# An emitter's engine clocks with GpSimd's hold on VectorE, new task priorities in the first mixer, and a last product in a place of its own

## The chip, the cores and the metric

One core of a Trainium2 chip runs the whole kernel. The metric is device time in microseconds for one execution, lower is better. The core has five engines with instruction streams of their own, each in order: TensorE (PE in the profile, its weight loads PEld), VectorE (DVE), ScalarE (ACT), GpSimd (POOL) and SyncE (SP), which issues the DMAs.

## What is computed

A trunk of two layers on an input of 512 tokens by 1024 channels, float32. Layer 0 mixes tokens by four mLSTM heads and an S5 state space side by side, layer 1 by HGRN2; each layer ends in a SwiGLU channel mixer. Cut to what matters:

```python
for layer in range(2):
    h = rmsnorm(x, norm_g[layer, 0])
    mix = mixer_ab(h) if layer == 0 else mixer_c(h)
    x = x + rmsnorm(mix, norm_g[layer, 1])
    h = rmsnorm(x, norm_g[layer, 2])
    x = x + rmsnorm((silu(h @ w1) * (h @ w3)) @ w2, norm_g[layer, 3])

def mixer_ab(x):                                  # width 1024 -> 512 mLSTM, 512 gate, 512 S5
    xm, zm, us = split(x @ w_in)
    xc = silu(causal_dwconv(xm, conv_w, conv_b))
    q, k, v = blockwise(xc, wq), blockwise(xc, wk), blockwise(xm, wv)
    gates = concat(q, k, v) @ w_if + b_if
    out_m = (norm(mlstm(q, k, v, gates)) * mh_gain + skip * xc) * silu(zm)
    y = gelu(s5_ssm(us))                          # complex diagonal state space over positions
    out_s = y * sigmoid(y @ w_glu + b_glu)
    return concat(out_m, out_s) @ w_out

def mixer_c(x):
    q, f, i, g = split(x @ w_in)                  # 4 x 1024
    fg = lb + (1 - lb) * sigmoid(f)
    o = hgrn2(silu(q), 1 - fg, i, log(fg))        # 8 heads of 128, chunks of 64
    return (norm(o) * g_gain * silu(g)) @ w_out
```

## The kernel before

Everything stays in SBUF; weights stream in through SP's queue as `wraw` (512 KB a piece) and are split on the chip: ScalarE rounds `wraw` to `wh` (fp32r), VectorE or GpSimd makes `wl = wraw - wh`. Activations are split the same way into a high and a low part (`xh`, `xl`; `yh`, `yl`; `gh`, `gl`), and each product is three fp32r matmuls (high by high, low by high, high by low) of 128x512 into one PSUM bank. PSUM has four `bmm` banks, two `bs` and two `bm`, used in rotation.

The program runs mixer 0 (to about 231 us of the trace), SwiGLU 0 with its output phase (to about 616), mixer 1 (to about 880), SwiGLU 1, and a short tail. The parts overlap through tasks.

What sets the order is a Python emitter, class `Sched`. Each part of the program is a generator task with a priority number. The emitter keeps one modelled clock for each engine in `fr`; `mm`, `tp`, `tt`, `ts`, `stt`, `scan` and `act` emit one instruction and advance a clock by a cost written in them (`_go`). The next task is the one with the smallest key of three: the later of its wake time and the modelled PE clock, then its priority, then its wake time. `S.spawn(gen, wake, prio)` starts a task, `yield S.on(engine, t)` puts one back until an engine's clock has come near, `S.signal` and a yielded key tie tasks together. So costs and priorities together fix the order of the instructions on every engine, and with it which PSUM bank and which buffer each one has. `main()` has the lowest priority: the big projections `bmm<-xh,wh` and its two partners fill TensorE where nothing else is due. They are called the filler here. `Weights.task` asks the clocks of VectorE and GpSimd which of the two makes a `wl`.

In mixer 0 the names are these. `s5_setup` builds the S5 constants, `toeplitz` the kernel `TT` from `tts` (matmuls `bs<-p,tts` and copies). `s5_main` takes the four channel groups in turn: `bs<-X,WB` on PE, rotations and scans on VectorE (`t<-bs,Y` and on, ending in `xi` and `xr`), then a block of matmuls `X,TT`, `xr,WC`, `xi,WC` into one `bmm` bank, called the output block of a group here, and on ScalarE a gelu (`X<-bmm`), `yh`, and on VectorE `yl`. `mlstm` with its inner `head(h)` makes for each head a mask (`bmm<-negm,idb`, `bmm<-n,xh`), an Exp on ScalarE (`xh<-bmm`), and the score products (`bm<-xl,xc`). The GLU is the product `bmm<-yh,wh` and its partners. `post` normalises the mLSTM's chunks, `skip` and `evac` finish the results.

At the end of each phase the rows' mean squares go over PE (`bm<-mean,n`) to VectorE (`rstat`), to a power -0.5 on GpSimd (`rcol<-rstat,mhalf`), and by transposes back (`bm<-p,rcol`). In `last_out`, the end of SwiGLU 1, the closures made by `ev` evacuate the last sum as `Y`, ScalarE squares it with a row sum (`n<-Y`), VectorE multiplies `Y` by the gain in place (`Y<-Y,gb`), and a last `stt` makes `xh = Y * rcol + x`, which goes out by DMA.

## Time and profile before

| | |
|---|---|
| runs, us | 1236.94, 1237.29, 1232.99; median 1236.94 |
| the profiled execution, us | 1233.26; its span in the trace 1231.2 |
| mean granted TensorE clock | 0.991 |
| TensorE busy, us | 1197.5 (97 % of the span) |
| VectorE busy, us | 715.0 (58 %) |
| ScalarE busy, us | 524.6 (43 %) |
| GpSimd busy, us | 94.4 (8 %) |

Busy is time with an instruction running. The waits view says how long an engine stood idle ahead of a group of instructions, and which instruction of which engine ended that; the windows view gives busy time of each engine in a stretch and the granted TensorE clock (1.00 is the upper of its two levels, 2.4 GHz, 0.50 the lower, 1.2 GHz); the timeline lists instructions in order of start, with the idle time just ahead of each in brackets.

### The profile page before, as it was taken

To read this page: it belongs to the slowest core of one execution; us is meant where nothing else is said; L and a number is where in the kernel's file an instruction comes from. 1 tells how busy PE (TensorE), PEld (TensorE's weight loads), DVE (VectorE), ACT (ScalarE), POOL (GpSimd) and SP (SyncE) were. 2 spreads that over 40 slices of the span, in tenths; PEclk is the share of its full clock that TensorE was granted. 3 is DMA by queue.
4 is the path that set the end of the run, shared out by engine and by line. 5 is a ranking of instruction groups with operands and counts; after the bars stand their busy time and mean duration, and the time that the engine had idled before them with its cause. 6 is when DMAs were issued, how large, how long until landed. Compare 5 with 4: busy or idle time off the path is not lost.

```text
span 1231.2 us, 17078 instructions
## 1 busy us (share of the span) xinstructions
PE 1197.5 (97%) x6871; PEld 1016.0 (83%) x6871; DVE 715.0 (58%) x1206; ACT 524.6 (43%) x821; POOL 94.4 (8%) x96
## 2 busy tenths in 40 slices
PE   9998899999999999999999999999999999999997
PEld 8866789988888888889978787889888888888886
DVE  7999685963344434445876647755861454235533
ACT  5685575543423213233566455646541333024311
POOL 3100010000000000000122223310000000000000
PEclk9998899999999999999999999999999999999999
DMA  6301015132333322333042132222241243025301
GB/s 230 102 21 36 2 35 164 68 122 83 120 92 97 103 91 97 103 91 116 19 131 72 61 97 69 86 86 87 90 167 52 86 154 121 18 75 160 125 18 52
DMA packets 33902, 110.67 MB, mean 90 GB/s; under 512 B 3744, under 2 KB 4128, under 8 KB 33824
## 3 DMA queue, kind: packets, MB, share of 16 engines
q1 hardware_dynamic: 33824, 109.59, 27.5%
q8 instruction: 54, 0.88, 0.3%
q14 instruction: 24, 0.20, 0.1%
HBM read 107.47 MB, written 2.10 MB: 89 GB/s over the span
## 4 chain that ended last, share of the span: by engine, by line
PE 80%; DVE 13%; ACT 3%; issue 1%; POOL 1%; DMA 0%; SPq 0%; DVEq 0%; POOLq 0%; ACTq 0%
PE bmm L158 76%; PE bm L158 2%; DVE wl L178 2%; PE bs L158 2%; DVE t L178 2%; DVE n L178 1%; PE bm L162 1%; DVE n L190 1%; ACT wh L172 1%; DVE Y L178 1%; DVE t L194 1%; DVE xc L190 1%; POOL rcol L180 1%; ACT L170 1%; DMA wraw<-in_W_dram 0%
## 5 line engine op out<-in xcount | busy, mean ns | idle before, releaser
L158 PE MATMUL bmm<-xh,wh 128*128 128x512 f32 (+1 forms) x1008 | 383.5, 380 | 0.7 <-DVE Y L178 0.7
L158 PE MATMUL bmm<-xl,wh 128*128 128x512 f32 (+1 forms) x1008 | 378.8, 376 | 0.4 <-DVE xl L190 0.4
L158 PE MATMUL bmm<-xh,wl 128*128 128x512 f32 (+1 forms) x1008 | 378.6, 376 | 0.0
L172 ACT ACTIVATE wh<-wraw 128x1024 fp32r<-128x1024 f32 (+2 forms) x181 | 182.9, 1013 | 360.7 <-PE bmm L158 249.0
L178 DVE TENSOR_TENSOR wl<-wraw,wh 128x1024 fp32r<-128x1024 f32 (+2 forms) x180 | 211.3, 1176 | 100.4 <-ACT wh L172 99.8
L158 PEld LDWEIGHTS bmm<-xh,wh 128*128 128x128 f32 x1008 | 190.9, 189 | 34.6 <-issue 2.3
L158 PEld LDWEIGHTS bmm<-xh,wl 128*128 128x128 f32 x1008 | 190.9, 189 | 34.3
L158 PEld LDWEIGHTS bmm<-xl,wh 128*128 128x128 f32 x1008 | 191.0, 190 | 33.2 <-DVE xl L190 0.8
L178 DVE TENSOR_TENSOR a<-bmm,n 128x512 f32<-128x512 f32 x86 | 59.0, 690 | 184.3 <-PE bmm L158 182.1
L178 DVE TENSOR_TENSOR Y<-bmm,Y 128x512 f32<-128x512 f32 (+1 forms) x36 | 22.7, 630 | 94.7 <-PE bmm L158 94.7
L158 PE MATMUL bmm<-gh,wh 128*128 128x512 f32 (+1 forms) x160 | 60.6, 379 | 0.0
L158 PE MATMUL bmm<-gl,wh 128*128 128x512 f32 (+1 forms) x160 | 60.5, 378 | 0.0
L158 PE MATMUL bmm<-gh,wl 128*128 128x512 f32 (+1 forms) x160 | 60.5, 378 | 0.0
L180 POOL TENSOR_TENSOR rcol<-rstat,mhalf 128x2 f32<-128x2 f32 (+1 forms) x10 | 11.7, 1172 | 498.1 <-DVE rstat L186 498.1
L158 PE MATMUL bmm<-woh,gh 128*128 128x512 f32 x120 | 46.9, 391 | 0.0
L158 PE MATMUL bmm<-woh,gl 128*128 128x512 f32 x120 | 46.7, 389 | 0.0
L158 PE MATMUL bmm<-wol,gh 128*128 128x512 f32 x120 | 46.7, 389 | 0.0
L172 ACT ACTIVATE a<-a 128x512 f32<-128x512 f32 x44 | 27.4, 623 | 34.5 <-DVE a L178 34.3
L172 ACT ACTIVATE gh<-a 128x512 fp32r<-128x512 f32 x44 | 27.6, 631 | 33.2 <-DVE a L178 32.6
L172 ACT ACTIVATE xh<-X,p 128x256 fp32r<-128x256 f32 (+1 forms) x56 | 29.9, 537 | 26.2 <-DVE X L178 23.9
L170 ACT ACT_TABLE_LOAD x28 | 35.9, 1283 | 0.5
L158 PEld LDWEIGHTS bmm<-gh,wh 128*128 128x128 f32 x160 | 30.1, 188 | 5.7
(369 smaller groups left out, 1923.0 us busy)
## 6 DMA issues: line engine op xcount, KB each, us to landing
wraw<-in_W_dram SPq DMA_DIRECT2D x179, 512.0 KB, 3.5
wraw<-in_W_dram SPq DMA_DIRECT2D x18, 256.0 KB, 2.7
X<-in_x_dram SPq DMA_DIRECT2D x16, 256.0 KB, 4.2
wraw<-in_W_dram SPq DMA_DIRECT2D x8, 384.0 KB, 3.0
out_dram<-xh SPq DMA_DIRECT2D x8, 256.0 KB, 2.0
setb<-in_s5bc_dram SPq DMA_DIRECT2D x1, 512.0 KB, 5.7
gb<-in_gb_dram SPq DMA_DIRECT2D x1, 512.0 KB, 3.3
p<-in_p_dram SPq DMA_DIRECT2D x1, 226.5 KB, 5.6
```

The source lines that it names most:

```text
L158: self.nc.tensor.matmul(out, lhsT=lhsT, rhs=rhs, start=start, stop=stop, skip_group_check=True)
L162: self.nc.tensor.transpose(out, in_, ident)
L170: self.nc.scalar.preload_act_table_set(t)
L172: self.nc.scalar.activation(out=out, in_=in_, func=func, scale=scale, bias=bias)
L178: self.nc.vector.tensor_tensor(out=out, in0=in0, in1=in1, op=op)
L180: self.nc.gpsimd.tensor_tensor(out=out, in0=in0, in1=in1, op=op)
L190: self.nc.vector.scalar_tensor_tensor(out=out, in0=in0, scalar=scalar, in1=in1, op0=op0, op1=op1)
L194: self.nc.vector.tensor_tensor_scan(out, d0, d1, 0.0, op0, op1)
```

## The change

First, the emitter's model. VectorE instructions with both operands in SBUF (`held`) are modelled to end only after a GpSimd instruction that would run beside them. An fp32r matmul right behind one that is not fp32r, or behind a transpose, costs 0.087 us more. GpSimd's `tt`, power and `ts` have new costs. Second, priorities of mixer 0's tasks have new numbers. Third, in `last_out` the product goes to `z`, a tile of its own, and the last `stt` reads `z`; the square still reads `Y`.

```diff
@@ class Sched
+        self.hold = []
+        self.dense = True
-    def _go(self, eng, after, cost):
+    def _go(self, eng, after, cost, held=False):
         s = max(self.fr[eng], after, self.w)
         if eng == "v" and cost < 0.15 and after == 0.0:
             cost += 0.06
+        if held:
+            for a, b in self.hold:
+                if a < s + cost - 0.1 and s < b:
+                    s = max(s, b - cost + 0.1)
         self.fr[eng] = s + cost
+        if eng == "g" and cost > 0.3:
+            self.hold = self.hold[-7:] + [(s, s + cost)]
@@ mm, tp
-        return self._go("pe", after, p * n / 2300.0 if lhsT.dtype != F32R else n * 0.000428 + 0.0085)
+        cost = p * n / 2300.0 if lhsT.dtype != F32R else n * 0.000428 + 0.0085
+        if lhsT.dtype == F32R and not self.dense:
+            cost += 0.087
+        self.dense = lhsT.dtype == F32R
+        return self._go("pe", after, cost)
...
+        self.dense = False
@@ tt, ts, stt
-            return self._go("v", after, n / 960.0 + 0.07)
+            return self._go("v", after, n / 960.0 + 0.07, held=not (self.psum(in0) or self.psum(in1)))
-        return self._go("g", after, n * (0.00176 if op == ALU.mult and len(in0.shape) > 2 else 0.0022) + (0.2 + 0.17 * n if op == ALU.pow else 0.1))
+        return self._go("g", after, 0.35 + 0.17 * n + (0.4 if n == 4 else 0.0) if op == ALU.pow else n * 0.0024 + 0.1)
-        ... if eng == "v" else n * 0.00096 + 0.1)
+        ... if eng == "v" else n * 0.0026 + 0.1)
@@ last_out
+                z[i, f] = self.pt(f"xl{2 * i + f}")
-                t = S.tt(y, y, self.gb[:, 512 * f:512 * f + 512], ALU.mult, after=t)
+                S.tt(z[i, f], y, self.gb[:, 512 * f:512 * f + 512], ALU.mult, after=t)
...
-                t1 = S.stt(o, self.Y[:, 2 * i + f], r[:, 2:3], px[f][0], ALU.mult, ALU.add, after=t)
+                t1 = S.stt(o, z[i, f], r[:, 2:3], px[f][0], ALU.mult, ALU.add, after=t)
@@ mixer 0, the priorities that differ in value
-        S.spawn(self.rotations(fp), wake=S.fr["v"], prio=1)
+        S.spawn(self.rotations(fp), wake=S.fr["v"], prio=1.05)
-            S.spawn(turn(z, t), wake=t, prio=2)
+            S.spawn(turn(z, t), wake=t, prio=1.5)
-        S.cur[1] = 0.95
-        S.spawn(self.toeplitz(), prio=0.9)
+        S.cur[1] = 0.6
+        S.spawn(self.toeplitz(), prio=0.85)
-        S.spawn(values(), prio=0.8)
-        S.spawn(queries(), prio=1.15)
+        S.spawn(values(), prio=1.0)
+        S.spawn(queries(), prio=0.9)
-        S.spawn(head(0), prio=1.2)
-        S.spawn(head(1), prio=1.2)
+        S.spawn(head(0), prio=0.95)
+        S.spawn(head(1), prio=0.6)
-                    S.spawn(head(h), prio=1.2)
+                    S.spawn(head(h), prio=1.15)
-            S.spawn(self.post(fp, i, pn, po, gate[:, i], t, to), wake=t, prio=1)
+            S.spawn(self.post(fp, i, pn, po, gate[:, i], t, to), wake=t, prio=1.05)
-        S.spawn(self.ml_setup(fp), prio=0.85)
-        S.spawn(self.s5_main(fp), prio=1)
-        S.spawn(self.mlstm(fp), prio=1.05)
-        S.spawn(self.skip(), prio=1.1)
+        S.spawn(self.ml_setup(fp), prio=0.95)
+        S.spawn(self.s5_main(fp), prio=0.6)
+        S.spawn(self.mlstm(fp), prio=1.1)
+        S.spawn(self.skip(), prio=0.6)
-                        S.spawn(self.evac(evu(s, ps, t), key), wake=t, prio=0.6)
+                        S.spawn(self.evac(evu(s, ps, t), key), wake=t, prio=0.7)
-                S.spawn(self.conv(j, t), wake=t, prio=0.75)
+                S.spawn(self.conv(j, t), wake=t, prio=0.95)
```

What the new numbers do to the order is seen in the two programs' instruction streams. TensorE has the same instructions in both. ScalarE has 36 loads of its function tables instead of 29, three of the seven more in mixer 0 and four in mixer 1. One `wl` goes from VectorE to GpSimd. The line of a helper differs in the two files: a matmul is L158 before and L167 in the change, a VectorE `tt` L178 and L192.

The first place is on TensorE, where mixer 0's filler runs out. `p,tts` are the Toeplitz matmuls, `X,WB` those that begin an S5 group, `xc,n` and `p,K` lead to the heads' queries and keys, and `xh,wh` with its two partners is the filler. Before:

```order
L158 MATMUL bmm_1132<-xh_273,wh 128x512
L158 MATMUL bmm_1132<-xl_274,wh 128x512
L158 MATMUL bmm_1132<-xh_273,wl 128x512
L158 MATMUL bs_1211<-X,WB_776 64x128 x8
L158 MATMUL bs_1222<-X,WB_776 64x128 x8
L158 MATMUL bmm_1132<-xh_281,wh 128x512
L158 MATMUL bmm_1132<-xl_282,wh 128x512
L158 MATMUL bmm_1132<-xh_281,wl 128x512
L158 MATMUL bmm_1132<-xh_293,wh 128x512
L158 MATMUL bmm_1132<-xl_294,wh 128x512
L158 MATMUL bmm_1132<-xh_293,wl 128x512
L158 MATMUL bm_1265<-xc,n_543 128x512
```

In the change:

```order
L167 MATMUL bmm_1131<-xh_276,wh 128x512
L167 MATMUL bmm_1131<-xl_277,wh 128x512
L167 MATMUL bmm_1131<-xh_276,wl 128x512
L167 MATMUL bm_1175<-xc,n_524 128x512
L167 MATMUL bs_1183<-X,WB_752 64x128 x8
L167 MATMUL bs_1184<-X,WB_752 64x128 x8
L167 MATMUL bm_1209<-xc,n_524 128x512
L167 MATMUL bm_1219<-xc,n_524 128x512
L167 MATMUL bs_1222<-p_124,tts 64x128 x8
L167 MATMUL bm_1237<-xc,n_524 128x512
L175 MATMUL bm_1247<-p_124,K_616 128x68 x4
```

The last filler stood behind the `X,WB` of the second S5 group and behind all `p,tts`; now it stands ahead of both, and the `p,tts` stand among the matmuls of the queries and heads.

The second place is on TensorE too, from the last S5 output block to the GLU (`yh,wh`). Before:

```order
L158 MATMUL bmm_1547<-xr_1456,WC_168 32x128 x4
L158 MATMUL bmm_1547<-xi_1457,WC_1123 32x128 x4
L158 LDWEIGHTS idb
L158 MATMUL bmm_1597<-negm,idb 128x512
L158 MATMUL bmm_1545<-n_628,xh_1516 128x128 x4
L158 MATMUL bmm_1597<-n_628,xh_1517 128x128 x4
L158 MATMUL bm_1614<-xl_1264,xc 128x128 x4
L158 MATMUL bm_1620<-xl_1394,xc 128x128 x4
L158 MATMUL bmm_1626<-yh_1390,wh 128x512
```

In the change:

```order
L167 MATMUL bmm_1574<-xr_1427,WC_168 32x128 x4
L167 MATMUL bmm_1574<-xi_1428,WC_1109 32x128 x4
L175 MATMUL bm_1623<-p_124,xc 128x128 x4
L167 LDWEIGHTS idb
L167 MATMUL bmm_1636<-negm,idb 128x512
L175 MATMUL bm_1640<-p_124,xc 128x128 x4
L167 LDWEIGHTS idb
L167 MATMUL bmm_1646<-negm,idb 128x512
L167 MATMUL bmm_1636<-n_617,xh_1633 128x128 x4
L167 MATMUL bmm_1646<-n_617,xh_1634 128x128 x4
L167 MATMUL bm_1663<-xl_1218,xc 128x128 x4
L167 MATMUL bm_1669<-xl_1236,xc 128x128 x4
```

Before, these are the products of heads 0 and 1, and those of heads 2 and 3 follow among the GLU's matmuls. In the change they are those of heads 2 and 3, and those of heads 0 and 1 stand ahead of the last output block, head 1's even ahead of the first.

The third place is the junction of mixer 0 and SwiGLU 0, the operands of the first half of the tokens, on VectorE (`rstat` holds the mean squares on their way to GpSimd's power). Before:

```order
L190 SCALAR_TENSOR_TENSOR n_2389<-Y,p_123,n_2352 128x256
L178 TENSOR_TENSOR X<-X,n_2388 128x256
L190 SCALAR_TENSOR_TENSOR xl_2493<-X,p_123,xh_2492 128x256
L178 TENSOR_TENSOR wl<-wraw,wh 128x1024
L186 TENSOR_SCALAR rstat<-bm_2571 128x2
L190 SCALAR_TENSOR_TENSOR n_2389<-Y,p_123,n_2352 128x256
```

On GpSimd, in the change:

```order
L194 TENSOR_TENSOR mst<-mst,mhalf 128x4 x4
L194 TENSOR_TENSOR rcol<-rstat,mhalf 128x2
L194 TENSOR_TENSOR wl<-wraw,wh 128x1024
L194 TENSOR_TENSOR rcol<-rstat,mhalf 128x2
L194 TENSOR_TENSOR rcol<-rstat,mhalf 128x4
```

The `wl` in VectorE's fourth row is now GpSimd's third, between the powers of the two halves, and TensorE's `bm<-mean,n` of the second half stands nine matmuls later.

## Rows read from the trace of the kernel before

**Rows 1.** The page's busy time of each engine: us, share of the span, instructions.

```profile
PE 1197.5 (97%) x6871; PEld 1016.0 (83%) x6871; DVE 715.0 (58%) x1206; ACT 524.6 (43%) x821; POOL 94.4 (8%) x96
```

**Rows 2.** The waits of TensorE: us in total, times, longest us.

```profile
PE bmm L158 <- DVE xr L178: 5.2, 1, 5.2
PE bm L162 <- DVE n L178: 3.3, 2, 1.8
...
PE bm L162 <- POOL rcol L180: 2.0, 4, 0.5
PE bmm L158 <- DVE osl L178: 1.9, 1, 1.9
```

**Rows 3.** Windows: us, busy us and (instructions) of each engine, clock, DMA.

```profile
100.00:140.00 40.00, 33.52 (x534) 25.87 (x538) 36.83 (x69) 21.20 (x34) 0.24 (x3) 0.89 0.07 21
136.00:140.00 4.00, 3.03 (x60) 3.06 (x64) 3.42 (x7) 0.00 (x0) 0.00 (x0) 0.50 0.00 0
140.00:180.00 40.00, 37.81 (x273) 33.44 (x266) 27.38 (x97) 27.34 (x59) 4.14 (x3) 0.98 0.05 15
400.00:500.00 100.00, 100.00 (x443) 82.81 (x442) 40.52 (x46) 24.88 (x28) 0.00 (x0) 1.00 0.30 98
```

**Rows 4.** Timeline of TensorE, 113 to 146 us: start us, us, instruction, [idle before].

```profile
113.13 0.40 PE L158 MATMUL bmm<-xh,wl 128*128 128x512 f32 x1
...
116.31 0.40 PE L158 MATMUL bmm<-X,TT 128*32 128x128 f32 x8
116.53 0.40 PE L158 MATMUL bmm<-xr,WC 128*32 128x128 f32 x8
...
136.97 0.66 PE L158 MATMUL bmm<-xr,WC 128*32 128x128 f32 x8 [5.16 <-DVE xr L178]
...
141.62 0.39 PE L158 MATMUL bmm<-negm,idb 128*128 128x512 bf16 x1
...
145.33 0.47 PE L158 MATMUL bmm<-yh,wh 128*128 128x512 f32 x1
```

**Rows 5.** Timeline of VectorE, three rows of the S5 groups.

```profile
111.11 2.48 DVE L178 TENSOR_TENSOR t<-bs,Y 128x512 f32<-128x512 f32 x4 [1.33 <-PE bs L158]
...
126.48 0.69 DVE L178 TENSOR_TENSOR t<-bs,Y 128x512 f32<-128x512 f32 x1 [0.81 <-PE bs L158]
...
136.15 0.68 DVE L178 TENSOR_TENSOR xr<-t,t 128x508 f32<-128x508 f32 x1
```

**Rows 6.** Timeline of ScalarE behind the last S5 output block.

```profile
142.93 0.63 ACT L172 ACTIVATE yh<-X 128x512 fp32r<-128x512 f32 x1
143.57 1.28 ACT L170 ACT_TABLE_LOAD   x1
144.87 1.09 ACT L172 ACTIVATE xh<-bmm 128x512 f32<-128x512 f32 x2
```

**Rows 7.** Timeline at the junction of mixer 0 and SwiGLU 0, TensorE and VectorE.

```profile
225.51 0.69 PE L158 MATMUL bm<-mean,n 128*128 128x1 f32 x5 [1.46 <-DVE n L178]
...
226.41 1.21 DVE L178 TENSOR_TENSOR wl<-wraw,wh 128x1024 fp32r<-128x1024 f32 x1
```

**Rows 8.** Timeline of mixer 1: one VectorE operation twice, and GpSimd.

```profile
732.11 2.42 POOL L180 TENSOR_TENSOR wl<-wraw,wh 128x1024 fp32r<-128x1024 f32 x1 [0.49 <-ACT wh L172]
...
732.97 2.10 DVE L178 TENSOR_TENSOR f<-f,em 128x512 f32<-128x512 f32 x1 [0.23 <-ACT em L172]
...
744.97 0.69 DVE L178 TENSOR_TENSOR f<-f,em 128x512 f32<-128x512 f32 x1
```

**Rows 9.** Timeline of TensorE at SwiGLU 0's operands, the scales' transposes.

```profile
249.84 0.43 PE L162 MATMUL bm<-p,rcol 128*128 128x128 f32 x2 [0.55 <-POOL rcol L180]
```

**Rows 10.** Timeline of the tail.

```profile
1224.78 0.19 ACT L784 ACTIVATION_READ_ACCUMULATOR n<-Y 128x1 f32 x1
1225.00 0.69 DVE L178 TENSOR_TENSOR Y<-Y,gb 128x512 f32<-128x512 f32 x1 [0.85 <-ACT n L784]
1225.61 0.15 DVE L178 TENSOR_TENSOR rcol<-rstat 128x1 f32<-128x1 f32 x1
```

More of the change, by code (lines that the diff above doesn't have):

```diff
@@ L178, in tt, with psum @@
             self.nc.vector.tensor_tensor(out=out, in0=in0, in1=in1, op=op)
-            return self._go("v", after, n / 960.0 + 0.07)
+            return self._go("v", after, n / 960.0 + 0.07, held=not (self.psum(in0) or self.psum(in1)))
         self.nc.gpsimd.tensor_tensor(out=out, in0=in0, in1=in1, op=op)
-        return self._go("g", after, n * (0.00176 if op == ALU.mult and len(in0.shape) > 2 else 0.0022) + (0.2 + 0.17 * n if op == ALU.pow else 0.1))
+        return self._go("g", after, 0.35 + 0.17 * n + (0.4 if n == 4 else 0.0) if op == ALU.pow else n * 0.0024 + 0.1)
+    @staticmethod
+    def psum(ap):
+        return "b" == ap.tensor.name[0] and ap.tensor.name[1] in "ms"
     def ts(self, out, in0, s1, op0, s2=None, op1=ALU.bypass, after=0.0, eng="v"):
@@ L186, in ts @@
         e.tensor_scalar(out=out, in0=in0, scalar1=s1, scalar2=s2, op0=op0, op1=op1)
-        return self._go(eng, after, n / 1530.0 + (0.065 if isinstance(s1, float) else 0.12) if eng == "v" else n * 0.00096 + 0.1)
+        return self._go(eng, after, n / 1530.0 + (0.065 if isinstance(s1, float) else 0.12) if eng == "v" else n * 0.0026 + 0.1)
     def stt(self, out, in0, scalar, in1, op0, op1, after=0.0):
         self.nc.vector.scalar_tensor_tensor(out=out, in0=in0, scalar=scalar, in1=in1, op0=op0, op1=op1)
-        return self._go("v", after, self._n(out) / 960.0 + 0.13)
+        return self._go("v", after, self._n(out) / 960.0 + 0.13, held=not (self.psum(in0) or self.psum(in1)))
     def scan(self, out, d0, d1, op0, op1, after=0.0):
@@ L770, in last_out @@
         ss = self.pt("rstat", (128, 4), bufs=2), self.pt("rstat", (128, 4), bufs=2)
+        z = {}
         def ev(i, f):
@@ L1939, in mixer0 @@
                         yield 0
-                S.spawn(self.evac(evo(2 * g + mm)(ps, None, t), key), wake=t, prio=1)
+                S.spawn(self.evac(evo(2 * g + mm)(ps, None, t), key), wake=t, prio=1.0)
             self.W.release(i)
@@ L2082, in build @@
             S.spawn(K.lower_bound(), prio=3)
-            S.spawn(main(), prio=5)
+            S.spawn(main(), prio=5.0)
             S.run()
```

## The prediction

> **What bounds the kernel now.** I began with the page's busy times: TensorE runs 97 % of the span, VectorE 58 %, ScalarE 43 % [rows 1]. The change takes no work from TensorE, so it can gain only what TensorE waits, or what it runs below its full clock. The waits of TensorE come next: they are scattered, and the longest is 5.2 us, for the `xr` of the last S5 group [rows 2]. The windows tell why: from 100 to 140 us VectorE is busy 36.83 of 40 and TensorE 33.52, while between 400 and 500 us TensorE is busy without a break, 443 matmuls in 100 us, 0.226 each [rows 3]. So the feed-forward parts have nothing to give; mixer 0 from 80 to 140 is bound by VectorE's chain, and the rest is single waits at junctions and in mixer 1. In TensorE's timeline the reader sees the filler end at 113.13, the wait of 5.16 us, and the last S5 output block behind it, from 136.97 to 141.62, at half the pace: eleven groups of eight matmuls in 4.65 us, 0.42 each, where a group of an earlier block took 0.22 (116.31 to 116.53) [rows 4]. The granted clock of that stretch was 0.50, the 1.2 GHz level [rows 3].
>
> All sums below are against the profiled execution, 1233.26 us. That is 3.7 under the median of the runs, 1236.94.
>
> **Mixer 0.** Before, the products of heads 0 and 1 follow the last S5 block, from 141.62 to 145.33, 3.7 us [rows 4]. In the change they stand ahead of that block, and so inside time in which TensorE waits for `xr`. The work left behind the wait is 3.7 us shorter: that is the main term. Heads 2 and 3 now stand ahead of the GLU rather than in it; that is the same work in another order and costs nothing by itself.
>
> When `xr` comes is VectorE's matter. Ahead of it, VectorE waited 1.33 us for the `X,WB` of the second group, which stood behind filler, and 0.81 for that of another [rows 5]. In the change the filler runs on without breaks and ends ahead of the second group's `X,WB`, and the Toeplitz matmuls stand behind it, so TensorE comes to it earlier; I take both waits as gone: 2.1 us. Against that, by the two VectorE orders with the durations of before, 0.9 us more head work stands ahead of the last `xr` than `yl` and other work leaves. That makes it 1.2 us earlier at best; at worst the new order of banks costs as much again. I take 0.7. Mixer 0 gains 3.7 + 0.7 = 4.4 us, with nothing and 7.5 as ends: nothing if the time comes back at the next late thing, the GLU's `osl` (1.9 us now [rows 2]; VectorE has 12.6 us free from 140 to 180 [rows 3]); 7.5 if the last block also runs at the full clock (12 groups, 0.2 saved on each, 2.4 us) and `xr` comes 1.2 early.
>
> ScalarE gets three more table loads here. A load took 1.28 us and the next activation began 1.30 after the load's start, with none lost ahead of it [rows 6]. So 3.9 us go on an engine that is free for 18.8 of the 40 us from 100 to 140 [rows 3]: nothing, as long as no load stands between the last output block and its `yh`. The Trainium skill ("ScalarE: Activation LUTs", What ACT_TABLE_LOAD costs) puts a switch of tables at about 2.66 us, load and drain together. By that the three would be 8.0 us, and if half of it lay ahead of the last gelu the gain of 4.4 would be about 0.4. The row shows the load and no drain, so I keep 1.30.
>
> **Junction of mixer 0 and SwiGLU 0.** TensorE waited 1.46 us for VectorE's `n` ahead of `bm<-mean,n`; one `wl` of 1.21 us stands in VectorE's stream just behind [rows 7]. The `mean,n` matmuls now stand nine matmuls later and the `wl` is GpSimd's. The wait of 1.46 should go; but on GpSimd a `wl` took 2.42 us, and a VectorE operation beside it 2.10 instead of 0.69 [rows 8], so up to 1.41 comes back on VectorE, and the second half's power is queued behind the `wl`. I take half the wait, 0.7, with -2.4 and +3 as ends.
>
> **Scales' transposes.** At three junctions `bm<-p,rcol` now stands three 256-wide matmuls later; it waited 0.55 us for GpSimd at each [rows 9], and the waits for `rcol` are four in all [rows 2]. A 256-wide matmul is half of 0.226, so three cover 0.34: 1.0 us in all, between nothing and 1.65.
>
> **Mixer 1.** Nothing is set there by hand; only the new costs act. The two waits of 3.3 us together [rows 2] are at the transposes `bm<-p,n` of the fourth and fifth head. In TensorE's order the fourth moves 66 rows later, the fifth 15, which at 0.226 is 3.4 us and covers its 1.8. But later transposes make later outputs, four more table loads stand on ScalarE, and the second head's work starts some 10 us later. I take half, 1.6, between -1 and +3.3.
>
> **Tail.** The gain's product waited 0.85 us for ScalarE's square and began at 1225.00; `rcol` followed at 1225.61, though the row sum was there at 1224.97 [rows 10]. With a place of its own the product is done before 1224.97, so `rcol` starts near 1225.0: 0.6 us, all on the path. The bound on the other side is nothing.
>
> **Sum.** 4.4 + 0.7 + 1.0 + 1.6 + 0.6 = 8.3, so 1225.0 against the profiled execution. Two of the four times before lie near 1233.1 and two near 1237.1, so a median may land on either; I add the half, 1.9, and forecast **1226.9 us**. Its own range is 1222 to 1231.
>
> **The rivals.** About 0.5 % (6.2 us) is what a measurement of this kernel can tell from no change.
>
> *The waits come back.* VectorE stays busy over nine tenths up to 140 us [rows 3], and what TensorE no longer waits for `xr` it waits for `osl` or a head's mask. For it: the sum of VectorE's work is the same, less one `wl`. Against it: VectorE's free time from 140 to 180. Mixer 0 gains nothing and mixer 1 nothing: 0.7 + 1.0 + 0.6 = 2.3, 1231.0 + 1.9 = about 1232.9.
>
> *More than forecast.* The last block runs at the full clock and all of mixer 1's waits go: 2.4 + 1.7 more, and the rest of the junction 0.8: 13.2 in all, 1220.1 + 1.9 = 1222, or near 1220 without the added half.
>
> *TensorE thins out and slows: slower.* With the filler spent earlier, TensorE has only small matmuls between waits for longer than before (12 us by my estimate from the orders), and in such a stretch it was granted 0.50 [rows 3]. If it is held there, three output blocks ahead of the last take 2.4 us more each, 7.3, and the heads' 3.7 us double: 11 us on one engine. It decides once that is more than the slack ahead of the fourth group's `X,WB`, which I estimate from the orders at 2.7 us: then `xr` comes 8.3 late, less the 3.7 moved ahead of it, plus 3.9 if the three table loads then stand in the chain of the gelus, and what the other parts give is 2.3: +6.2, 1239.5, with 1.9 about 1241. Against it: at 114 to 117 us, with two blocks back to back, the pace was the full one [rows 4].
>
> *GpSimd's hold at the junction.* The operand chain of the first half is held for 1.41 us and the power waits 2.42 behind the `wl`, both on the path: the junction loses 2.4 instead of gaining 0.7, so 1226.9 + 3.1 = 1230. For it: the one pair of rows [rows 8]. The Trainium skill ("SBUF — State Buffer", SBUF: two separate sides) says that VectorE and GpSimd take one shared port pair as an exclusive lock for a whole instruction, the loser blocked. By that rule the 2.10 us is no accident, and the move would cost here whatever VectorE then has to do with both operands in SBUF. Against it: VectorE's `wl` of 1.21 us is gone from the same stretch.
>
> **How the numbers follow.** Forecast 0.45, more 0.15, hold 0.12, waits back 0.18, slower 0.10. Faster by over 6.2 us (under 1230.7) holds nine tenths of the forecast, all of "more" and half of "hold": 0.62. Slower is its rival alone: 0.10; the same 0.28. The range from 1218.5 to 1236 leaves out "slower" and the tails.
>
> **What the trace would show.** Right: heads 0 and 1 (`bmm<-n,xh`) ahead of the last `X,TT` block, the wait for `xr` under 2 us where TensorE works, the last `xr` at 135 to 137, the GLU started by 143, `mean,n` without a wait, `rcol` in the tail right behind the row sum. Wrong: a granted clock at the lower level through 102 to 137 with `xr` after 138; a wait for `osl` or `Y` of over 4 us; mixer 1's span no shorter.

## The result and the profile after

| | before | change |
|---|---|---|
| median of the runs, us | 1236.33 (1232.99 to 1237.29, 4 runs) | 1223.12 (1220.80 to 1224.76, 4 runs) |
| the profiled execution, us | 1233.26 | 1222.88 |
| span in the trace, us | 1231.2 | 1220.9 |
| mean granted TensorE clock | 0.991 | 0.995 |

The change is faster: ratio 0.990, interval 0.9886 to 0.9914. Against the profiled execution of before, on which the sum was made, it is 10.4 us; between the medians 13.2, because that execution lay at the fast end of its runs.

Where the time went is read off marks that both programs have: the start of the same work on TensorE in the two traces, and by how much the change is ahead there. (At `mean,n` of the second half the places differ a little: in the change nine matmuls more, 1.1 us, lie ahead of it.)

| mark | before | change | ahead, us |
|---|---|---|---|
| first GLU matmul (`yh,wh`) | 145.33 | 144.94 | 0.4 |
| first matmul behind the GLU (`osh,wh`) | 169.34 | 163.65 | 5.7 |
| first matmul of mixer 0's output product | 196.99 | 190.07 | 6.9 |
| `mean,n` of the second half, junction | 225.51 | 219.72 | 5.8 |
| `p,n` behind SwiGLU 0's first operands | 246.18 | 240.43 | 5.8 |
| second `mean,n` at the end of SwiGLU 0 | 594.45 | 588.60 | 5.9 |
| second `mean,n` at the end of mixer 1 | 860.93 | 851.61 | 9.3 |
| last instruction's end | 1228.08 | 1217.81 | 10.3 |

So 5.7 us come from mixer 0, a further 1.2 from the stretch behind the GLU are given back by the junction (50.4 us from the output product to `p,n`, where it took 49.2), mixer 1 gives about 3.5 and the end 1.0. The GLU starts hardly earlier, but heads 2 and 3 are done by then.

These marks are of one execution each. Two kernels of the experiments below differ from the change only at the junction: e9, with its `wl` back on VectorE, and e11, with eight small matmuls more. Up to there TensorE has the same instructions in the same order. In their traces the GLU starts at 145.71 and 148.07 and the first matmul behind it at 164.44 and 166.79, so there mixer 0 is 4.9 and 2.5 us ahead of before, not 5.7.

The waits of TensorE in the change (us in total, times, longest):

```profile
PE bmm L167 <- DVE xr L192: 3.1, 1, 3.1
PE bs L167 <- DVE t L192: 2.2, 3, 1.2
PE bm L167 <- DVE n L192: 1.8, 2, 1.1
PE bmm L167 <- DVE xh L204: 1.7, 1, 1.7
PE bm L175 <- POOL rcol L194: 1.3, 4, 0.8
```

The wait for `xr` was 5.2 and is 3.1. Those for `osl` (1.9) and for `n` at `p,n` (3.3) are no longer among them [rows 2]; the 1.8 for `n` here is at `mean,n`. The wait for `rcol` fell from 2.0 to 1.3. New is 1.7 us for `xh`, a head's operand.

Windows of the change (us, busy us and instructions of PE, PEld, DVE, ACT and POOL, the granted clock, DMA):

```profile
100.00:140.00 40.00, 34.60 (x596) 28.18 (x594) 39.48 (x75) 27.49 (x41) 0.24 (x3) 1.00 0.08 28
136.00:140.00 4.00, 2.45 (x88) 2.37 (x88) 3.96 (x8) 0.81 (x2) 0.00 (x0) 1.00 0.02 6
140.00:180.00 40.00, 39.49 (x244) 34.03 (x237) 30.24 (x113) 31.27 (x69) 5.15 (x4) 1.00 0.08 27
220.00:224.00 4.00, 3.88 (x22) 3.58 (x22) 3.82 (x7) 1.87 (x6) 2.54 (x1) 0.63 0.17 25
```

From 100 to 140 us VectorE worked 39.48 us instead of 36.83, and the clock was 1.00 instead of 0.89; from 136 to 140 it was 0.50 and is 1.00 [rows 3]. At the junction, 220 to 224, it is 0.63.

TensorE around the last S5 output block:

```profile
134.01 0.40 PE L167 MATMUL bmm<-X,TT 128*32 128x128 f32 x8
137.55 0.42 PE L167 MATMUL bmm<-xr,WC 128*32 128x128 f32 x8 [3.13 <-DVE xr L192]
137.76 0.43 PE L167 MATMUL bmm<-xi,WC 128*32 128x128 f32 x8
...
140.58 0.38 PE L167 MATMUL bmm<-negm,idb 128*128 128x512 bf16 x1
...
144.94 0.48 PE L167 MATMUL bmm<-yh,wh 128*128 128x512 f32 x1
```

and VectorE's last `xr`:

```profile
136.72 0.68 DVE L192 TENSOR_TENSOR xr<-t,t 128x508 f32<-128x508 f32 x1
```

TensorE still waits for it, 3.13 us, but the block then runs at 0.22 us for eight matmuls (137.55 to 137.76), where it took 0.42 [rows 4]. What follows is the products of heads 2 and 3, and the GLU at 144.94. The last `xr` itself is later than before, 136.72 against 136.15 [rows 5].

The full pace belongs to this execution, not to the order. In e9 and e11 the same matmuls waited 3.12 us for the same `xr`, and the block behind the wait ran at the lower clock. The row of e9:

```profile
136.84 0.66 PE L167 MATMUL bmm<-xr,WC 128*32 128x128 f32 x8 [3.12 <-DVE xr L192]
```

and a window of e9 and one of e11, with a clock of 0.57 and 0.50:

```profile
136.00:140.00 4.00, 3.16 (x62) 3.19 (x66) 4.00 (x8) 0.14 (x1) 0.00 (x0) 0.57 0.02 6
138.00:142.00 4.00, 4.00 (x80) 4.00 (x83) 3.14 (x6) 0.00 (x0) 0.00 (x0) 0.50 0.01 4
```

At the junction, TensorE:

```profile
219.72 1.02 PE L167 MATMUL bm<-mean,n 128*128 128x1 f32 x8 [1.10 <-DVE n L192]
...
221.27 0.41 PE L167 MATMUL bmm<-xl,wh 128*128 128x256 f32 x1
221.48 0.41 PE L167 MATMUL bmm<-xh,wl 128*128 128x256 f32 x1
```

and GpSimd and VectorE:

```profile
219.82 2.72 POOL L194 TENSOR_TENSOR wl<-wraw,wh 128x1024 fp32r<-128x1024 f32 x1 [12.23 <-ACT wh L186]
...
220.48 2.34 DVE L208 SCALAR_TENSOR_TENSOR xl<-X,p,xh 128x256 fp32r<-128x256 f32 x1 [0.18 <-ACT xh L186]
222.74 0.47 DVE L208 SCALAR_TENSOR_TENSOR n<-Y,p,n 128x256 f32<-128x256 f32 x1
```

The wait for `n` is 1.10, where it was 1.46 [rows 7], and the 256-wide matmuls behind it start 0.21 us apart, at half the pace, until 224. That is nothing new: before, the clock fell behind the same matmuls, to 0.58 from 226 to 230 us.

```profile
226.00:230.00 4.00, 4.00 (x23) 4.00 (x23) 3.82 (x10) 2.42 (x7) 1.20 (x1) 0.58 0.32 108
```

The `wl` that moved took 2.72 us on GpSimd, and an `xl` beside it 2.34 instead of the 0.47 or 0.48 that its neighbours take: a hold of 1.9 us. It ends 0.28 us after the `wl`. The Trainium skill ("SBUF — State Buffer", SBUF: two separate sides) says that when a GpSimd operation and a VectorE operation with two inputs in SBUF meet, the one that starts first has the shared port pair for its whole instruction and the other is blocked. The trace agrees as to the wait, though 0.28 us behind the `wl` is less than the 0.47 of an `xl` by itself.

In mixer 1, the two transposes that waited, of the fourth and fifth head, before:

```profile
697.10 0.66 PE L162 MATMUL bm<-p,n 128*128 128x128 f32 x4 [1.47 <-DVE n L178]
...
753.83 0.66 PE L162 MATMUL bm<-p,n 128*128 128x128 f32 x4 [1.80 <-DVE n L178]
```

and in the change, without a wait:

```profile
703.64 0.60 PE L175 MATMUL bm<-p,n 128*128 128x128 f32 x4
...
746.95 0.60 PE L175 MATMUL bm<-p,n 128*128 128x128 f32 x4
```

The tail:

```profile
1214.51 0.69 DVE L192 TENSOR_TENSOR xl<-Y,gb 128x512 f32<-128x512 f32 x1
...
1215.11 0.19 ACT L803 ACTIVATION_READ_ACCUMULATOR n<-Y 128x1 f32 x1
1215.33 0.16 DVE L192 TENSOR_TENSOR rcol<-rstat 128x1 f32<-128x1 f32 x1
```

`rcol` now starts right behind the row sum, 1.54 us behind the start of the last `Y` (1213.79); before it was 2.15 behind it (1223.46), at 1225.61 [rows 10].

### The profile page after: what moved, and what is told of

It reads as the page before. It is cut to its first block, busy times and chain, and to the rows that moved or that the text cites. A ratio compares the mean times of both kernels' runs of the same rounds, so it can differ in the third digit from the quotient of the medians.

```text
span 1220.9 us, 17069 instructions
## 1 busy us (share of the span) xinstructions
PE 1197.1 (98%) x6871; PEld 1014.1 (83%) x6871; DVE 716.0 (59%) x1205; ACT 534.8 (44%) x828; POOL 96.5 (8%) x97
## 4 chain that ended last, share of the span: by engine, by line
PE 81%; DVE 12%; ACT 3%; issue 2%; DMA 1%; POOL 1%; SPq 0%; DVEq 0%; POOLq 0%; ACTq 0%
PE bmm L167 77%; PE bm L167 2%; DVE t L192 2%; DVE wl L192 2%; DVE n L192 1%; PE bm L175 1%; DMA wraw<-in_W_dram 1%; DVE t L212 1%; PE bs L167 1%; DVE n L208 1%; DVE xl L208 1%; ACT wh L186 1%; POOL rcol L194 1%; DVE Y L192 1%; ACT n L186 1%
## 5 line engine op out<-in xcount | busy, mean ns | idle before, releaser
L167 PE MATMUL bmm<-xh,wh 128*128 128x512 f32 (+1 forms) x1008 | 383.6, 381 | 0.0
L167 PE MATMUL bmm<-xl,wh 128*128 128x512 f32 (+1 forms) x1008 | 379.3, 376 | 0.9 <-DVE xl L208 0.8
L167 PE MATMUL bmm<-xh,wl 128*128 128x512 f32 (+1 forms) x1008 | 379.0, 376 | 0.0
L192 DVE TENSOR_TENSOR wl<-wraw,wh 128x1024 fp32r<-128x1024 f32 (+2 forms) x179 | 209.2, 1171 | 95.2 <-ACT wh L186 94.7
L167 PEld LDWEIGHTS bmm<-xl,wh 128*128 128x128 f32 x1008 | 191.4, 190 | 34.4 <-DVE xl L208 1.9
L167 PEld LDWEIGHTS bmm<-xh,wl 128*128 128x128 f32 x1008 | 191.0, 189 | 34.6
L167 PEld LDWEIGHTS bmm<-xh,wh 128*128 128x128 f32 x1008 | 191.2, 190 | 33.7 <-DVE Y L192 0.2
L192 DVE TENSOR_TENSOR a<-bmm,n 128x512 f32<-128x512 f32 x86 | 59.1, 691 | 182.2 <-PE bmm L167 179.9
L192 DVE TENSOR_TENSOR Y<-bmm,Y 128x512 f32<-128x512 f32 (+1 forms) x36 | 22.7, 632 | 99.8 <-PE bmm L167 99.8
L167 PE MATMUL bmm<-gh,wh 128*128 128x512 f32 (+1 forms) x160 | 60.6, 379 | 0.0
L167 PE MATMUL bmm<-gl,wh 128*128 128x512 f32 (+1 forms) x160 | 60.5, 378 | 0.0
L167 PE MATMUL bmm<-gh,wl 128*128 128x512 f32 (+1 forms) x160 | 60.5, 378 | 0.0
L167 PE MATMUL bmm<-woh,gh 128*128 128x512 f32 x120 | 46.9, 391 | 0.0
L167 PE MATMUL bmm<-woh,gl 128*128 128x512 f32 x120 | 46.7, 389 | 0.0
L167 PE MATMUL bmm<-wol,gh 128*128 128x512 f32 x120 | 46.7, 389 | 0.0
L186 ACT ACTIVATE a<-a 128x512 f32<-128x512 f32 x44 | 27.4, 623 | 33.2 <-DVE a L192 32.9
L167 PEld LDWEIGHTS bmm<-gh,wh 128*128 128x128 f32 x160 | 30.1, 188 | 5.7
```

Of the source, the lines that this page charges most:

```text
L167: self.nc.tensor.matmul(out, lhsT=lhsT, rhs=rhs, start=start, stop=stop, skip_group_check=True)
L186: self.nc.scalar.activation(out=out, in_=in_, func=func, scale=scale, bias=bias)
L192: self.nc.vector.tensor_tensor(out=out, in0=in0, in1=in1, op=op)
```

## The experiments

First the three parts of the change by themselves, then the costs one by one, then single steps. All are timed against the kernel before on the same chip; the change stands at 0.990.

### The parts alone

The tail's edit alone:

```diff
+                z[i, f] = self.pt(f"xl{2 * i + f}")
-                t = S.tt(y, y, self.gb[...], ALU.mult, after=t)
+                S.tt(z[i, f], y, self.gb[...], ALU.mult, after=t)
```

> The kernel before with the tail's edit alone (the product in a place of its own). Theory: the row operations of the tail start at the row sum's end, 0.6 us earlier (0.4 to 1.0), and nothing else moves, so 1236.3 becomes about 1235.7, which timing alone can't tell; the tail's rows show it. Rival: the product still waits for ScalarE (they share something else than Y), the tail's rows keep their distances and the gain is nothing.

1233.94 us, ratio 0.9988 (0.9979 to 0.9997). The distance from the last `Y` to `rcol` is 1.54 us in its trace, as in the change. That is the 0.6 us; the rest of the 1.4 between the medians is within the interval.

The emitter's new costs alone, all priorities as before (everything in the diff's `Sched` parts):

> The kernel before with the emitter's new costs alone, old priorities. The heads' products stay behind the last S5 output block. Theory (the gain is made of places): mixer 1 takes the order of the change and its 3.1 us; the scales' transposes give some 0.6; mixer 0 keeps its wait for xr and the half clock behind it: 4 us faster than before in all. Rival (the costs place mixer 0's heads too): 7 us or more, and the wait for xr is under 4 us.

1230.93 us, ratio 0.9968 (0.9955 to 0.9980): 4.4 us between the medians, as the theory had it. Its mixer 1 (from the mark at 594.53 to that at 857.92) took 263.4 us, like the change's 263.0 and unlike the 266.5 of before. Its output product and its junction are within 0.3 us of before (second `mean,n` at 225.79). Its mixer 0 is another than expected: the wait for `xr` is 0.96 us, but TensorE waits 2.29 for `setb` ahead of it, the last block still runs at the lower clock (0.50 from 136 to 140 us), and the first matmul behind the GLU is 0.9 later than before (170.26). The rival's short wait came without the rival's gain.

The new priorities alone, the costs as before (everything in the diff's mixer 0 part):

> The kernel before with the new priorities alone, old costs. Products of heads 0 and 1 stand ahead of the last S5 block. Theory: mixer 0's 5 to 6 us come from here (3.7 of work inside the wait, about 2 from a clock that stays up, less 0.5 for a later xr), mixer 1 gives nothing: 5.5 us faster, 1231. Rival (without the hold in the costs the emitter is wrong about VectorE and xr comes later still): 2 us or less.

1240.63 us, ratio 1.0040 (1.0028 to 1.0052): slower, by 5.2 us. That `xr` comes later still is the rival's; a loss is more than either had. The heads do stand ahead of the last block, and yet `xr` comes at 145.01. TensorE's row on the way there:

```profile
125.55 0.71 PE L162 MATMUL bm<-p,K 68*128 68x68 f32 x4 [4.36 <-ACT xl L172]
```

and the window around it:

```profile
124.00:132.00 8.00, 6.45 (x33) 6.03 (x35) 5.87 (x11) 4.39 (x9) 0.00 (x0) 0.57 0.00 0
```

`bm<-p,K` waited 4.36 us for ScalarE, where two loads of the function tables and three other activations (120.03 to 124.92) stood ahead of the `xl` in question. Behind it the clock was 0.57, and VectorE, which has no break there in the change (7.96 of the same 8 us), was busy 5.87: it waited above all for the next group's `X,WB`, which stood in TensorE's stream behind all that.

The three parts by themselves give -0.12, -0.32 and +0.40 %, about nothing in sum; together they give -1.0 %. The next three take one cost at a time out of the change.

Without the list of holds:

```diff
-        if eng == "g" and cost > 0.3:
-            self.hold = self.hold[-7:] + [(s, s + cost)]
```

> The change without the list of GpSimd's holds in the emitter; all else as in the change. The order of mixer 0 is then another one: filler among the Toeplitz matmuls, heads 0 and 1 behind the last S5 block. Theory: mixer 0 loses most of its 5.7 us and the time is 1227 to 1231; in mixer 1 the waits of the transposes stay away, since the other costs move them too. Rival (the hold's cost matters in mixer 1 alone, where GpSimd works): mixer 0 as in the change, mixer 1 as before, 1226.

1236.23 us, ratio 1.0006 (0.9996 to 1.0017): all of the gain is gone, in mixer 1 too (267.7 us). The waits of TensorE in it:

```profile
PE bm L160 <- ACT xl L179: 4.2, 1, 4.2
PE bmm L160 <- DVE xr L185: 3.0, 1, 3.0
PE bm L160 <- DVE Y L185: 2.5, 1, 2.5
PE bm L168 <- DVE n L185: 2.5, 2, 1.4
```

The wait for `n` of `bm<-p,n` (L168) is back with 2.5 us, and mixer 0 has a new one of 4.2 for ScalarE's `xl`. My expectation was 1227 to 1231, the rival 1226; more is lost than either.

Without the 0.087 us for an fp32r matmul behind one that isn't:

```diff
-        if lhsT.dtype == F32R and not self.dense:
-            cost += 0.087
```

> The change without the 0.087 us for an fp32r matmul behind one that isn't. The order of mixer 0 is another: the filler lasts until the GLU, heads 0 and 1 stand behind the last S5 block with filler between, VectorE has four operations fewer ahead of the last xr. Theory (any work in the wait is as good as the heads'): xr about 2.5 us earlier than in the change, no long wait and no fall of the clock, within 3 us of the change: 1222 to 1226. Rival (the priorities fit only the one set of costs, and some in-order wait of several us stands somewhere else): 1229 or more.

1234.73 us, ratio 0.9993 (0.9984 to 1.0002), the rival's side. The filler lasts until 143 us, but it doesn't fill the wait, since the last block's first matmuls stand ahead of it in the stream:

```profile
138.00 0.66 PE L167 MATMUL bmm<-xr,WC 128*32 128x128 f32 x8 [8.12 <-DVE xr L187]
```

Mixer 1 took 264.3 us, so this cost mattered in mixer 0 above all.

With GpSimd's old `tt` and power costs, the hold kept:

```diff
-        return self._go("g", after, 0.35 + 0.17 * n + (0.4 if n == 4 else 0.0) if op == ALU.pow else n * 0.0024 + 0.1)
+        return self._go("g", after, n * (0.00176 if op == ALU.mult and len(in0.shape) > 2 else 0.0022) + (0.2 + 0.17 * n if op == ALU.pow else 0.1))
```

> The change with GpSimd's old tt and power costs, the hold kept. Heads 0 and 1 stand between the second and third S5 block, still ahead of the last. Theory (the heads' place decides): mixer 0 within 2 us of the change, the transposes' waits in mixer 1 partly back, 1224 to 1227. Rival (as for the costs of dense matmuls): 1229 or more.

1235.85 us, ratio 1.0005 (0.9996 to 1.0015), again the rival's side. The heads stand ahead of the last block here, and it didn't help:

```profile
PE bs L167 <- DVE tts L192: 3.9, 1, 3.9
PE bm L175 <- DVE n L192: 3.6, 2, 2.6
PE bmm L167 <- DVE xr L192: 3.6, 1, 3.6
```

The Toeplitz matmuls wait 3.9 us for `tts`, and the transposes of mixer 1 3.6 (it took 267.7 us).

### The heads and the wait

The change with the heads' priorities of before:

```diff
-        S.spawn(head(0), prio=0.95)
-        S.spawn(head(1), prio=0.6)
+        S.spawn(head(0), prio=1.2)
+        S.spawn(head(1), prio=1.2)
...
-                    S.spawn(head(h), prio=1.15)
+                    S.spawn(head(h), prio=1.2)
```

> The change with the heads' priorities of before (1.2 for all four). Their products then stand just ahead of the last S5 output block, still inside TensorE's wait, and VectorE has five operations fewer ahead of the last xr. Theory (what counts is that the 3.7 us stand ahead of the block, and when xr comes): xr about 2 us earlier than in the change, the time 1 to 2.5 us under it, about 1221.5. Rival (head 1's early place among the Toeplitz matmuls is what keeps TensorE and its clock busy): slower than the change, 1226 or more.

1229.54 us, ratio 0.9956 (0.9942 to 0.9969): 6.4 us slower than the change. The theory's first half came true and its second did not; the number is the rival's, but the trace shows another reason than the rival's. VectorE:

```profile
133.70 0.68 DVE L192 TENSOR_TENSOR xr<-t,t 128x508 f32<-128x508 f32 x1
...
137.29 0.88 DVE L204 TENSOR_SCALAR xh<-G,p 128x512 f32<-128x512 f32 x2
```

TensorE:

```profile
137.83 3.78 PE L167 MATMUL bmm<-n,xh 128*128 128x128 f32 x16 [10.06 <-DVE xh L204]
```

`xr` came at 133.70, 3.0 us earlier than in the change. But the heads' matmuls `n,xh` stand ahead of the block, and the `xh<-G` that they read stands on VectorE behind `xr` and other work, at 137.29. TensorE waited 10.06 us for it with the block behind, whose operands were there. Work placed ahead of a wait takes time out of it only where its own operands come before those that are waited for.

The change with the matmuls of heads 0 and 1 held until the last block has been emitted:

```diff
             tl = S.ts(L, G, self.sel[:, 58 + h:59 + h], ALU.mult)
+            if h < 2:
+                yield "s5last"
             pd, kd = yield from self.alloc("mm")
@@ s5_out, behind its matmuls
+        if j == 3:
+            S.signal("s5last", 0.0)
```

> The change with the matmuls of heads 0 and 1 held until the last S5 output block has been emitted, so that they stand behind it as before; mixer 1 is that of the change. Theory: the 3.7 us come back, less 1 to 1.5 for two or three VectorE operations fewer ahead of xr, plus up to 2.2 if the longer wait lets the clock fall: 3 to 5 us slower than the change, 1226 to 1228. Rival (mixer 0's gain lies in the filler and the Toeplitz matmuls, not in the heads): within 1.5 us of the change.

1224.70 us, ratio 0.9914 (0.9899 to 0.9929): 1.6 us behind the change by the medians, with overlapping intervals: less than the 3 to 5 expected, and about the rival's 1.5. TensorE:

```profile
135.82 0.65 PE L167 MATMUL bmm<-xr,WC 128*32 128x128 f32 x8 [6.20 <-DVE xr L192]
136.22 0.68 PE L167 MATMUL bmm<-xi,WC 128*32 128x128 f32 x8
```

and windows:

```profile
136.00:140.00 4.00, 4.00 (x80) 4.00 (x78) 3.27 (x6) 0.00 (x0) 0.00 (x0) 0.50 0.01 4
220.00:224.00 4.00, 2.47 (x22) 2.30 (x21) 3.90 (x11) 3.87 (x10) 0.00 (x0) 1.00 0.16 65
```

The wait is 6.20 us, the clock behind it 0.50 and the block at the slow pace again: `xr` is 1.7 us earlier (134.99), the rest as expected. Its first matmul of the output product starts at 194.19, 4.1 us behind the change. But the second `p,rcol` of the junction starts at 226.94, only 1.3 behind the change's 225.67. Here the clock stays 1.00 at the junction, where the change has 0.63, and a wait of 0.78 us for `rcol` ahead of it is absent.

The 4.1 us hold for the change's profiled execution, whose block ran at the full clock. In the traces of e9 and e11, with the change's order and the lower clock, the output product starts at 190.83 and 193.18, only 3.4 and 1.0 us ahead of this one. From the last `xr` to the output product it took 60.8 us before, 59.2 here, and 53.4, 54.8 and 56.1 in the change, e9 and e11; against that, `xr` comes 1.0 to 2.1 us later in those three. So the heads' place is worth 1 to 4 us at the output product, and 2.8 us of the gain there (196.99 before) are left without it. In the time its worth is not clear of the noise.

The kernel before with 22 matmuls that fill the wait and whose result is overwritten:

```diff
         ps, key = yield from self.alloc("mm")
+        for _ in range(22 if j == 3 else 0):
+            S.nc.tensor.matmul(ps..., lhsT=self.idb, rhs=self.negm..., start=True, stop=True, ...)
```

> The kernel before with 22 matmuls of 128x512 bf16, whose result is overwritten, ahead of the last S5 output block, where TensorE waits for xr: work in the wait that is worth nothing but activity. Theory (the wait lowers the clock): the wait is under 1 us, the granted clock from 136 to 140 us is 1.00, the last block takes 2.6 us instead of 4.7, the heads behind it some 0.5 less, 2 to 2.5 us faster in all, 1234. Rival (the block is slow for a reason of its own, such as operands that arrive late): it still takes 4.7 us and the time is that of before.

1234.53 us, ratio 0.9993 (0.9984 to 1.0002). TensorE:

```profile
134.99 4.91 PE L1480 MATMUL bmm<-negm,idb 128*128 128x512 bf16 x22
139.83 0.43 PE L158 MATMUL bmm<-X,TT 128*32 128x128 f32 x8
...
142.03 0.43 PE L158 MATMUL bmm<-X,TT 128*32 128x128 f32 x8
```

and the window:

```profile
136.00:140.00 4.00, 4.00 (x27) 1.73 (x24) 3.93 (x8) 0.26 (x1) 0.00 (x0) 1.00 0.00 0
```

The clock is 1.00, and the block ran from 139.83 at 0.22 us for eight. From the last `xr` to the GLU it took 7.1 us (139.46 to 146.54), where before took 9.2 (136.15 to 145.33): the 2.1 us are there. In the time only 0.9 show, and the interval holds nothing. In the profiled execution the wait for `osl` (1.90 us) was followed by eight matmuls at 0.43 us, which in that of before ran at the full pace, so part went there. Another part was lost ahead of the edit, on the instructions of before: the last group's `X,WB` took 3.52 us (127.42) instead of 1.96, at a clock of 0.58 from 127 to 131 us, and `xr` came at 139.46. Whether that holds for the other runs is open.

### The junction

The change with its one `wl` on VectorE again (e9), the emitter's clocks advanced as for GpSimd, so that nothing else moves:

```diff
+                if i in (32, 33) and pool and not S.alone:
+                    S.nc.vector.tensor_tensor(out=l[:, c], in0=r[:, c], in1=h[:, c].bitcast(F32), op=ALU.subtract)
+                    t2 = S._go("g", t1, n * 0.0024 + 0.1)
```

> The change with the junction's one wl on VectorE again; the emitter's clocks are advanced as if it were GpSimd's, so every other instruction keeps its place. Theory (at the junction the two prices are alike: 1.2 us of VectorE against a hold of about 1.4): within 1 us of the change. Rival (GpSimd's hold costs the junction 2 to 3 us): 1221. Other rival (the move is what shortens the junction): 1225.

1222.66 us, ratio 0.9894 (0.9877 to 0.9911): the same as the change. The hold is gone (every `xl` of the stretch takes 0.48 or 0.49 us). So the hold of 1.9 us is real and costs nothing that the intervals show, and neither does it show a gain that the `wl` is off VectorE.

The change with eight small matmuls ahead of the junction's second `mean,n` (e11):

```diff
+        self.nrc = getattr(self, "nrc", 0) + (nt == 2)
+        if nt == 2 and self.nrc == 2:
+            for q in range(8):
+                S.nc.tensor.matmul(ps[:, :128], lhsT=self.ident, rhs=self.ident, start=True, stop=True, ...)
```

> The change with eight fp32 matmuls of 128x128, whose result is overwritten, ahead of the second half's mean matmuls at the junction of mixer 0 and SwiGLU 0, where TensorE waits 1.1 us for n and then runs at the lower clock to 224 us. Theory (the fall of the clock there costs 1.5 us): the granted clock stays 1.00 from 220 to 224 us, 1 to 1.7 us faster than the change, about 1221.8. Rival (the stretch is bound by the operands of VectorE, not by the clock): the waits move to xl or rcol and the time is that of the change, 1223.

```profile
220.00:224.00 4.00, 4.00 (x38) 4.00 (x36) 3.71 (x11) 3.07 (x8) 0.92 (x1) 1.00 0.01 2
```

The clock stays at 1.00, and from `mean,n` to `p,rcol` it took 4.8 us instead of 6.0. But 1223.72 us, ratio 0.9905 (0.9889 to 0.9921), is the time of the change, as the rival had it. From the output product to `p,n` it took 49.9 us against 50.4, so 0.5 us is left of it: the added matmuls take their own time, and a wait of 0.40 us for `xl` follows. Its profiled execution was the slowest of five (1220.51 to 1226.25 us): its GLU started 3.1 us later than the change's, on the same instructions.

The same, with the keys' products held until the last `xr`:

```diff
+            yield ("cd", 3)
             yield S.on("v", max(t, tg))
             k_ = self.pt(f"xh{4 + i}")
```

> The same as e11, and the keys' products (xh<-bm,setb) held until the last xr has been emitted, so that VectorE has one operation less ahead of it. Theory: xr 0.6 to 0.7 us earlier and the last output block with it, and the junction as in e11: 1.5 to 2.3 us faster than the change, 1221. Rival (what was ahead of xr comes back behind it, ahead of the heads' masks): the same as e11.

1222.37 us, ratio 0.9902 (0.9889 to 0.9916). `xr` came at 135.44, 1.3 us earlier than in the change (0.7 of it there already at the third `xr`), yet the GLU at 146.00, 1.1 later: in VectorE's order one more of the keys' products then stands ahead of the second head's `xh<-G`. That is the rival. But the clock has a part in it that this run can't separate: behind a wait of 2.96 us the block ran at the slow pace from its third group on (0.60 from 136 to 140 us) and took 4.2 us, up to the next matmuls, instead of 2.5. No version here beats the change by more than its interval.

## Why the prediction was right, and where it was not

The direction and the range held; the gain was 1.25 times the forecast against the profiled execution (10.4 for 8.3). The total came out nearer than its parts: mixer 0 with the stretch behind it gave 6.9 for 4.4 and mixer 1 more than forecast, the junction lost 1.2 where 0.7 was to be gained, and part of the 6.9 is a clock that stayed up in the profiled execution and not in others. That much is luck. Of the signs I named, three did not come: the wait for `xr` is 3.13 us and not under 2, the GLU starts at 144.94 and not by 143, and `mean,n` waits 1.10. The 1.9 us that I added for the scatter of the runs were not needed: the change's runs lie around its profiled execution.

**Mixer 0 (forecast 4.4, range 0 to 7.5; measured 5.7).** The main term, the heads' 3.7 us inside the wait, is seen in the rows: from the last `xr` to the end of the GLU stretch before took 33.2 us (136.15 to 169.34) and the change 26.9 (136.72 to 163.65), 6.3 less, which is 3.7 plus the 2.2 of a block at the full clock (0.2 on each of the eleven groups behind the wait), and 0.4 more. In e9 and e11 it took 28.4 and 29.7, 4.8 and 3.5 less: about the 3.7, with little or nothing of the clock's part. With the heads held back, 1.0 to 4.1 us were lost by the output product, and 1.6 in the time. The clock's part I had only among the ends and in the rival "more than forecast"; it came in the change's trace and is no property of the order. (The upper end, 3.7 + 2.4 + 1.2, is 7.3 and not 7.5.) The step that failed is the 0.7 us for an earlier `xr`: both waits of VectorE did go, and its idle time from 100 to 140 us fell from 3.2 to 0.5, but the heads' and keys' work took all of it and more, and `xr` came 0.6 us later (in e9 0.1 earlier, in e11 0.9 later). I had put that work at 0.9 us. What I took for granted, that costs and priorities are parts of one gain, was wrong too: the first place's order of filler, Toeplitz and heads exists only with both, and in mixer 0 each half alone does little or harm. What makes the 2.8 us that stay with the heads held back, and which single priority carries them, was not tried one by one and stays open.

**Junction (forecast 0.7; measured a loss of 1.2, from 6.9 ahead at the output product to 5.8 at `p,n`).** The wait for `n` went from 1.46 to 1.10 only, one of 0.74 us for `Y` went, and new ones of 0.78 for `rcol` and 0.39 for `xl` came. The fall of the clock behind the second `mean,n` is no part of it, since before had it too. That is the wrong sign, but inside the bounds of -2.4 to 3.

**Scales' transposes (forecast 1.0).** The three waits of 0.55 us became 0.19, 0.18 and 0.19: 1.1 us at the places named. With the new 0.78 the sum of waits for `rcol` fell by 0.7 only.

**Mixer 1 (forecast 1.6; measured about 2.8).** Of the 3.5 us between the marks, 0.7 are two waits for `rcol` at its entry (0.34 and 0.55 before, none and 0.18 in the change), which belong to the scales' transposes. The two waits of 3.3 us went whole, only small ones grew (that for `f` from 0.46 to 0.81), and no price of the four more table loads shows. I halved a term whose both ends the order showed. The costs alone give it, and without the hold or GpSimd's costs the waits return.

**Tail (forecast 0.6; measured 0.6).**

**The rivals.** TensorE thinned out only a little: the last filler was at 104.41 against 113.13, it was still busy 34.60 us of the 40, and the granted clock was 1.00 (0.91 from 100 to 120 us in e9 and e11, as in before). What I had described as the slower case did occur, in the priorities alone: an in-order wait, the lower clock behind it, and VectorE starved. GpSimd's hold was there with 1.9 us and had no price that could be measured. A table load took 1.28 us (143.30) with the next activation 1.29 after its start (144.59), so the 1.30 of the rows stands, and the 2.66 that the Trainium skill ("ScalarE: Activation LUTs", What ACT_TABLE_LOAD costs) gives for a switch shows nowhere in the two traces: no load starts more than 0.03 us behind the activation ahead of it, and the next activation starts 1.29 to 1.34 us behind the load's start unless it waits for an operand.

## What to carry to other kernels

Priorities of a scheduler that works on modelled clocks are fitted to the model: test a corrected model and new priorities apart and together, since here the halves gave -0.3 and +0.4 % and the whole -1.0 %. Before work is moved into a wait of an in-order engine, check where its own operands are made; behind the awaited one, the wait grows (10 us instead of 3). And a gain read at one mark of one trace should be followed to the next junction, and looked for in a second trace of the same order: the heads' place was worth 4.1, 3.4 or 1.0 us at the output product, by the trace that was taken, and 1.6 in the time.

## What the runs showed of the hardware

The granted clock behind a wait of TensorE: after 5.16 us (before), 6.20 and 8.12 us it was at the lower level (1.2 GHz), about 0.42 us for eight of the small matmuls; with the wait filled it was at the upper (2.4 GHz), 0.22. After 3.13 us it was at the upper in the change's trace, and after 3.12 at the lower in those of e9 and e11, on the same instructions. At the junction it fell behind waits of 1.46 (before), 1.10 (the change) and 1.53 us (the costs alone, 0.59 from 226 to 230) and the eight one-column `mean,n`, and did not fall behind a wait of 1.53 at the same place in the kernel with the heads held back. So neither the length of a wait nor the order of the instructions fixed the clock here: a term of one to three microseconds came or went between executions of the same instructions (the GLU of the change's order started at 144.94, 145.71 and 148.07), and a sum by the rows of one trace can't be closer than that.
